# The FFN up projection of a hybrid diffusion trunk as a Strassen block product over pairs of token chunks

## The chip, the cores and the metric

One NeuronCore of one Trainium2 chip runs the kernel. The metric is the device time of one execution in microseconds, the median of three runs. Engines: PE multiplies matrices (PEld are its weight loads), DVE, ACT and POOL work elementwise on SBUF and PSUM, SP issues nearly all DMAs.

## The reference

One layer of a trunk with 128 context and 2048 latent tokens of width 1024, fp32. What matters here is the feed-forward block at its end, with FF = 2816:

```python
D_MODEL = 1024
D_FF = 2816
...
h = modulate(xs, g_norm2[l], sh2, sc2)
xs = xs + gt2[:, None, :] * conv_ffn(h, w_up[l], conv_w[l], conv_b[l], w_down[l])
...
#   x = x + gate2 * (SiLU(g) * val) @ w_down,  [g | val] = centred depthwise conv3(h @ w_up)
```

Context and latent tokens are separate sequences for the convolution. So `w_up` is 1024 x 5632: 22 blocks of 128 gate features and 22 of 128 value features, over 2176 tokens; the convolution takes each feature with its two neighbours in the token direction.

## The kernel before, in words

Every large product is made of three fp32r matmuls on hi/lo halves of the operands (`mm3`, L269 to L274): high by high, high by low, low by high. A half pair is made by an ACT copy to fp32r (the high half) and a DVE subtraction (the low half).

The kernel runs in stages: input projection with adaLN, state-space scan and attention, state-space output, merge, FFN up, FFN down. An instruction scheduler places each engine's instructions, from a program written stage by stage, so work of one stage may stand among another's.

The merge (`merge` L1010) goes over 17 tiles of 128 tokens. `turned` (L967) transposes the state-space half of a tile on PE (L972) and splits it (L974, L975); `merge_ssm` (L1045) multiplies by `wo` (24 matmuls of 512 columns, L273) and adds the result into x on DVE and POOL (L1053 to L1055); `h2_tile` (L1073) normalizes (`modulated_`, L246: L254 on DVE, transposes L259 on PE, modulation L265 on ACT) and `h2_split` (L1060) splits the tile into chunks H2 of 436 tokens plus a neighbour on each side: chunks 0 to 2 stay in SBUF, the tiles of chunks 3 and 4 go to DRAM (`hd`) and are split once the merge's memory is free. After ten tiles `merge` loads the first up weights.

`ffn_up` (L1089) takes 22 feature blocks fb times 5 chunks c. A pair of weight blocks [1024, 128], gate and value, is loaded and split once (`up_weights` L1080, L1085 on ACT, L1086 on DVE; 44 in all). One (fb, c) is two products of 24 matmuls over 438 columns (436 in the last chunk), 48 matmuls; 5280 in all. Each PSUM result becomes a convolution by three taps: ACT L1106, DVE L1108 and L1109; then tanh on ACT (L1112), two DVE products (L1113, L1114), and a DMA to `ffd` in DRAM. The first two feature blocks run over chunks 0 to 2 first, and stand partly in PE's gaps of the merge.

`ffn_down` (L1129) takes two halves of 11 feature blocks: 11 weight tiles (`down_weights`, L1125 and L1126), then per token tile a load from `ffd`, a split (L1139, L1140) and 66 matmuls of 512 columns in two or three banks, gated and added into x (L1152, L1153). `ffn_up` prepares the first `DW = 2` of its weights, and the gate rows of the down projection are made by PE transposes (`gate_rows`, L963).

```python
                    self.mm3(ps[:, :nn], lambda a, k: ws[fb][part][:, a, k, :],
                             lambda b, k: self.H2[c][:, b, k, :nn], 8)
```

## Time and profile before

| | |
|---|---|
| runs before | 2681.84, 2684.23, 2686.13 us; median 2684.23 |
| the profiled execution: span | 2684.1 us |
| PE busy, share of the span | 2531.3 us, 94% |
| PE weight loads | 2197.0 us, 82% |
| DVE | 1536.8 us, 57% |
| ACT | 1089.7 us, 41% |
| POOL | 727.8 us, 27% |

The profile shows one execution. An engine is busy while it executes an instruction; waiting, branching and issuing DMAs are not counted. The chain of waits goes back from the last instruction to whatever released each one. The clock granted to PE has two levels, 1.2 and 2.4 GHz; in the tables 1.00 is 2.4 GHz.

### The profile page before, as it was taken

The numbers are of one execution on the slowest core, as the hardware profiler recorded it, in microseconds if no ns is written. First come the engines' busy times: TensorE is split into PE (matmuls) and PEld (weight loads), VectorE is DVE, ScalarE is ACT, GpSimd is POOL, SyncE is SP. The second block draws the span as 40 slices with busy tenths as digits, with TensorE's granted clock in tenths as the row PEclk, the third lists the DMA queues.
The fourth block names the chain that finished last, engine by engine and source line by source line (L and its number), as shares of the span: only waits on it lengthen the run. The fifth ranks groups of instructions, "written<-read, shape, count | busy, mean of one in ns | idle before, by whom it ended". The sixth has DMA issues, their size and how long they took to land.

```text
span 2684.1 us, 34944 instructions
## 1 busy us (share of the span) xinstructions
PE 2531.3 (94%) x13046; PEld 2197.0 (82%) x13046; DVE 1536.8 (57%) x2576; ACT 1089.7 (41%) x2090; POOL 727.8 (27%) x1082
## 2 busy tenths in 40 slices
PE   6877997799999789999999999999999999999998
PEld 3756785688887567899999999999999988888887
DVE  6999767777776967654444444444444452224433
ACT  6544558777775666542222222222222230002111
POOL 1778105677776926500000000000000011111101
PEclk9988999899999899999999999999999999999999
DMA  8544745211112556641111111111111264344432
GB/s 247 166 144 159 231 133 188 93 66 66 66 62 80 123 181 223 215 154 55 40 55 40 40 55 40 55 40 40 55 39 48 61 202 132 107 131 139 124 115 74
DMA packets 245338, 287.20 MB, mean 107 GB/s; under 512 B 32058, under 2 KB 193202, under 8 KB 245042
## 3 DMA queue, kind: packets, MB, share of 16 engines
q1 hardware_dynamic: 240273, 276.07, 32.5%
q10 hardware_dynamic: 4896, 8.92, 1.0%
q8 instruction: 103, 1.69, 0.3%
q14 instruction: 66, 0.53, 0.1%
HBM read 183.08 MB, written 99.49 MB: 105 GB/s over the span
## 4 chain that ended last, share of the span: by engine, by line
PE 72%; DVE 6%; ACT 4%; issue 2%; DMA 1%; POOL 0%; SPq 0%; DVEq 0%; ACTq 0%; POOLq 0%
PE up L273 39%; PE dn L273 19%; PE pt L1003 3%; PE pm L273 2%; PE ps L851 2%; PE pt L879 2%; ACT HS L599 1%; PE po L883 1%; PE po L884 1%; DVE ha L682 1%; DVE pTl L890 1%; DVE sm L853 1%; DVE z L692 1%; ACT sm L840 0%; PE pst L596 0%
## 5 line engine op out<-in xcount | busy, mean ns | idle before, releaser
L273 PE MATMUL up<-H,upw 128*128 128x438 f32 (+1 forms) x5280 | 1058.9, 362 | 0.0
L273 PEld LDWEIGHTS up<-H,upw 128*128 128x128 f32 x5280 | 993.3, 188 | 61.0
L1108 DVE SCALAR_TENSOR_TENSOR cv<-up,vec,cv 128x436 f32<-128x436 f32 (+1 forms) x220 | 147.6, 671 | 455.9 <-ACT cv L1106 455.9
L1106 ACT ACTIVATE cv<-up,vec 128x436 f32<-128x436 f32 (+1 forms) x220 | 157.1, 714 | 575.1 <-PE up L273 575.1
L273 PE MATMUL dn<-dnw,aT 128*128 128x512 f32 (+1 forms) x1653 | 381.2, 386 | 0.0
L1153 POOL TENSOR_TENSOR xd<-xd,td 128x512 f32<-128x512 f32 x34 | 46.2, 1362 | 1225.5 <-DVE td L1152 1225.5
L273 PEld LDWEIGHTS dn<-dnw,aT 128*128 128x128 f32 x1653 | 307.7, 188 | 62.9
L1152 DVE TENSOR_TENSOR td<-dn,gate 128x512 f32<-128x512 f32 (+1 forms) x69 | 46.9, 683 | 288.4 <-PE dn L273 288.4
L187 DVE SCALAR_TENSOR_TENSOR wacc<-wa,scf,wacc 128x256 f32<-128x256 f32 x224 | 164.9, 777 | 10.1 <-ACT wacc L189 5.6
L1139 ACT ACTIVATE aT<-a 128x1408 fp32r<-128x1408 f32 x34 | 47.0, 1383 | 272.7 <-PE dn L273 261.2
L1109 DVE SCALAR_TENSOR_TENSOR cv<-up,vec,cv 128x436 f32<-128x436 f32 (+1 forms) x220 | 147.7, 671 | 7.5
L273 PE MATMUL dn<-upw,aT 128*128 128x512 f32 (+1 forms) x624 | 150.0, 385 | 0.0
L890 DVE TENSOR_TENSOR pTl<-pt,pTh 128x512 fp32r<-128x512 f32 x158 | 108.1, 684 | 51.7 <-ACT pTh L889 50.4
L273 PEld LDWEIGHTS dn<-upw,aT 128*128 128x128 f32 x624 | 115.6, 188 | 23.4
L853 DVE CUSTOM_DVE_ANT_0 sm<-ps,mask,nsink 128x640 f32<-128x640 f32 (+2 forms) x136 | 112.7, 830 | 29.7 <-PE ps L851 29.5
L840 ACT ACTIVATE sm<-sm,nm 128x640 f32<-128x640 f32 (+2 forms) x136 | 107.6, 791 | 27.4 <-DVE nm L853 27.2
L1112 ACT ACTIVATE th<-cv 128x436 f32<-128x436 f32 (+1 forms) x110 | 62.6, 569 | 135.1 <-DVE cv L1109 135.1
L1263 PE MATMUL aq<-win,hT 128*128 128x512 f32 x408 | 117.2, 423 | 0.0
L265 ACT ACTIVATE h<-tp,modc,G 128x128 f32<-128x128 f32 x272 | 100.1, 465 | 38.0 <-PE tp L259 33.5
L617 POOL TENSOR_TENSOR fm<-HS,A 128x544 f32<-128x544 f32 x64 | 91.8, 1435 | 86.5 <-ACT HS L599 70.7
L1263 PE MATMUL au<-win,hT 128*128 128x512 f32 x408 | 107.1, 405 | 7.1 <-DVE hT L1194 5.0
L879 PE MATMUL pt<-ident,sm 128*128 128x128 f32 x632 | 101.1, 279 | 12.4 <-ACT sm L840 7.6
(440 smaller groups left out, 3956.5 us busy)
## 6 DMA issues: line engine op xcount, KB each, us to landing
a<-ffd SPq DMA_DIRECT2D x34, 704.0 KB, 4.6
upraw<-in_w_up_dram SPq DMA_DIRECT2D x44, 512.0 KB, 3.8
ffd<-th SPq DMA_DIRECT2D x88, 218.0 KB, 1.9
xd<-x1d SPq DMA_DIRECT2D x34, 512.0 KB, 5.0
wa<-in_w_ada_dram SPq DMA_DIRECT2D x64, 256.0 KB, 3.1
dnraw<-in_w_down_dram SPq DMA_DIRECT2D x22, 512.0 KB, 5.2
qtd<-qT SPq DMA_DIRECT2D x17, 512.0 KB, 2.6
qT<-qtd SPq DMA_DIRECT2D x17, 512.0 KB, 3.9
```

The lines of the kernel that those rows point to most:

```text
L187: V.scalar_tensor_tensor(o, raw[:, k % RK], g, o, op0=OP.mult, op1=OP.add)
L265: S.activation(h[:, kk, :], pss[b][:, k, :], AF.Identity, scale=G[:, kk, st:st + 1], bias=self.modc[:, sh0 + kk, st:st + 1])
L273: self.T.matmul(ps, lhs(a, k), rhs(b, k), start=(first and k == 0 and n == 0), stop=(last and k == nk - 1 and n == 2))
L617: e.tensor_tensor(m, ev[:, :, ::-1] if n else ev, A[n], op=OP.mult)
L840: S.activation(out[hh][:, :W], out[hh][:, :W], AF.Exp, scale=-1.0, bias=nm[:, hh:hh + 1], accum_out=l[:, hh:hh + 1])
L853: V.tensor_tensor_reduce(t[:, :W], ps[:, c0:c0 + W], mask, -1.0, self.nsink[:, h:h + 1], op0=OP.add, op1=OP.min, accum_out=nm[:, hh:hh + 1])
L879: T.transpose(pt[:, hh], sm[hh][:, j * 128:(j + 1) * 128], self.ident)
L890: V.tensor_tensor(lo, pv, hi, op=OP.subtract)
L1106: S.activation(t[:, :n], ps[:, 1:1 + n], AF.Identity, scale=self.cw[1][:, j:j + 1], bias=self.cb[:, j:j + 1])
L1108: V.scalar_tensor_tensor(t[:, :n], ps[:, 0:n], self.cw[0][:, j:j + 1], t[:, :n], op0=OP.mult, op1=OP.add)
L1109: V.scalar_tensor_tensor(t[:, :n], ps[:, 2:2 + n], self.cw[2][:, j:j + 1], t[:, :n], op0=OP.mult, op1=OP.add)
L1263: T.matmul(t, hT[:, a, k, :], w[:, k, b, c0:c0 + t.shape[1]], start=(k + a + b == 0), stop=(k == 7 and a == 1))
```

## The change

The product [2176 tokens x 1024] by [1024 x 5632] becomes a block product. The operands of one unit are the four weight blocks a11, a12 (gate features, lower and upper half of the 1024 rows) and a21, a22 (value features), each 512 x 128, and the token blocks of two neighbouring chunks of 363 tokens (366 columns with their neighbours), each in two halves of the rows. Four block products would need 8 half products; the Strassen form (Winograd's, with 7) needs sums of the blocks of either side ahead, and sums of the products behind. Six chunks make three passes c of two chunks; 3 passes x 22 feature blocks are 66 units of 7 products of 12 matmuls over 366 columns, 5544 in all.

- `merge` (now L1017) no longer splits h; `h2_tile` (L1073) writes it to `hd` in DRAM, now [128, 8, 2184]. From tile 7 on it issues the token sums of pass 0 (`combos`), the operands of unit 0 and five of the seven token operands.
- `combos` (L1103): for each of four quarters, loads two chunks into a staging buffer, four POOL sums of 366 columns by L1114 to L1117, and a store to `td` in DRAM. Four steps a pass.
- `operand` (L1121): loads one of the seven token operands of a pass from `td` or `hd` by way of the same two staging buffers and splits it, in two instructions each of 2 x 366 columns on ACT (L1136) and DVE (L1137).
- `up_operands` (L1149): loads the two weight blocks of a feature block, four POOL sums S0 to S3 (L1155 to L1158) and seven splits of 512 elements: high halves on ACT (L1162), low halves (L1163) on DVE, one (`WP7`) on POOL. It does so in each unit.
- `ffn_up` (L1167): the products, copies of partial sums (`snap`, ACT), three DVE sums (L1237, L1246, L1258), the taps, and the gated product, whose last factor is a POOL product (L1199) as the value half of the convolution's vectors has been scaled by 0.5 in `vectors2`. PE's order in it is written by hand. At fb 18 and 21 of the first two passes the operands of the next pass are loaded.
- The down projection's pools open when those of the up projection are closed. Its weights are all loaded there, the gate rows come from DRAM (`gd`) by DMA, and the first token tile is loaded ahead of the weights.

The core of the diff:

```diff
+TOKENS = ((0, 0), (0, 2), (1, 1), (1, 0), (1, 2), (1, 3), (0, 3))
+WB7, WP7 = 9, (5,)
...
+        for o in (94, 138, 182, 226):
+            V.tensor_scalar(self.vec[:, o:o + 22], self.vec[:, o:o + 22], 0.5, None, op0=OP.mult)
...
+            if i == 7:
+                todo = self.combos(0)
+            if 7 <= i < 11:
+                next(todo)
+            if i == 8:
+                more = self.up_operands(0)
+            if 9 <= i < 16:
+                wts = next(more)
+            if 11 <= i < 16:
+                toks.append(self.operand(0, i - 11))
...
+    def combos(self, p):
+        G, Q = self.G, self.Q
+        for k in range(4):
+            t = self.stg.tile([128, 4, NR], F32, name="stg", bufs=2)
+            o = self.stg.tile([128, 4, NR], F32, name="stg", bufs=2)
+            for h in range(2):
+                c = NO * (2 * p + h)
+                Q.dma_start(t[:, h::2, :NI], self.hd.rearrange("q (b k) c -> q b k c", b=2)[:, :, k, c:c + NI])
+            tt = G.tensor_tensor
+            n = slice(0, NI)
+            tt(o[:, 0, n], t[:, 1, n], t[:, 0, n], op=OP.subtract)
+            tt(o[:, 1, n], t[:, 3, n], o[:, 0, n], op=OP.subtract)
+            tt(o[:, 2, n], t[:, 3, n], t[:, 1, n], op=OP.subtract)
+            tt(o[:, 3, n], t[:, 2, n], o[:, 1, n], op=OP.subtract)
+            Q.dma_start(self.td[p].rearrange("m q k c -> q m k c")[:, :, k], o[:, :, :NI])
+            yield
...
+    def operand(self, p, j):
+        n = 7 * p + j
+        pool, bufs = (self.tA, 5) if n % 9 < 5 else (self.tB, 4)
+        t = pool.tile([128, 2, 4, NR], F32R, name="T", bufs=bufs)
+        kind, m = TOKENS[j]
+        raw = self.stg.tile([128, 4, NR], F32, name="stg", bufs=2)
+        if kind:
+            self.Q.dma_start(raw[:, :, :NI], self.td[p, m])
+        else:
+            kh, h = divmod(m, 2)
+            c = NO * (2 * p + h)
+            self.Q.dma_start(raw[:, :, :NI], self.hd[:, 4 * kh:4 * kh + 4, c:c + NI])
+        for k in (0, 2):
+            src = raw[:, k:k + 2, :NI]
+            self.S.activation(t[:, 0, k:k + 2, :NI], src, AF.Copy)
+            self.V.tensor_tensor(t[:, 1, k:k + 2, :NI], src, t[:, 0, k:k + 2, :NI], op=OP.subtract)
+        return t
...
+    def up_operands(self, fb):
+        S, V, G, p = self.S, self.V, self.G, self.upw
+        g, v = self.up_raw(fb)
+        a11, a12, a21, a22 = g[:, 0:4], g[:, 4:8], v[:, 0:4], v[:, 4:8]
+        s = [p.tile([128, 4, 128], F32, name=f"S{n}", bufs=1) for n in range(4)]
+        G.tensor_tensor(s[0], a21, a22, op=OP.add)
+        G.tensor_tensor(s[1], s[0], a11, op=OP.subtract)
+        G.tensor_tensor(s[2], a11, a21, op=OP.subtract)
+        G.tensor_tensor(s[3], a12, s[1], op=OP.subtract)
+        out = []
+        for n, x in enumerate((a11, a12, s[1], s[0], s[2], a22, s[3])):
+            w = p.tile([128, 2, 4, 128], F32R, name="w", bufs=WB7)
+            S.activation(w[:, 0], x, AF.Copy)
+            (G if n in WP7 else V).tensor_tensor(w[:, 1], x, w[:, 0], op=OP.subtract)
+            out.append(w)
+            yield out
...
+    def ffn_up(self, first, p, pp):
+        Q, S, V, G = self.Q, self.S, self.V, self.G
+        units = [(c, fb) for c in range(3) for fb in range(22)]
+        o = slice(0, NO)
+        toks = {(0, j): t for j, t in enumerate(first[0])}
+        for j in range(5, 7):
+            toks[0, j] = self.operand(0, j)
+        wts = {0: first[1]}
+        for _ in first[2]:
+            pass
+        banks = {}
+        def product(u, j, bank, first=False):
+            w, t = wts[u][j], toks[units[u][0], j]
+            for k in range(4):
+                for n, (a, b) in enumerate(((0, 0), (0, 1), (1, 0))):
+                    self.T.matmul(bank[:, :NI], w[:, a, k], t[:, b, k, :NI], start=(first and k + n == 0),
+                                  stop=(k == 3 and n == 2), skip_group_check=True)
+        def taps(src, part, fb, name):
+            j = part * 22 + fb
+            t = p.tile([128, NO], F32, name=name, bufs=2)
+            S.activation(t, src[:, 1:1 + NO], AF.Identity, scale=self.cw[1][:, j:j + 1], bias=self.cb[:, j:j + 1])
+            V.scalar_tensor_tensor(t, src[:, 0:NO], self.cw[0][:, j:j + 1], t, op0=OP.mult, op1=OP.add)
+            V.scalar_tensor_tensor(t, src[:, 2:2 + NO], self.cw[2][:, j:j + 1], t, op0=OP.mult, op1=OP.add)
+            return t
+        def gated(g, v, c, fb):
+            th = p.tile([128, NO], F32, name="th", bufs=2)
+            S.activation(th, g, AF.Tanh, scale=0.5)
+            V.scalar_tensor_tensor(th, th, 1.0, g, op0=OP.add, op1=OP.mult)
+            G.tensor_tensor(th, th, v, op=OP.mult)
+            Q.dma_start(self.ffd[fb, :, NO * c:NO * c + NO], th)
+        def snap(x, name):
+            s = p.tile([128, NR], F32, name=name, bufs=2)
+            S.activation(s[:, :NI], x[:, :NI], AF.Copy)
+            return s
+        def begin(u):
+            x = pp.tile([128, 512], F32, name="X", bufs=3)
+            product(u, 0, x, True)
+            banks[u] = x, snap(x, "s1")
+        todo = []
+        begin(0)
+        for u, (c, fb) in enumerate(units):
+            x, s1 = banks.pop(u)
+            nxt = self.up_operands(units[u + 1][1]) if u + 1 < len(units) else iter(())
+            if fb in (4, 8, 12, 16) and c < 2:
+                if fb == 4:
+                    todo = self.combos(c + 1)
+                next(todo)
+            y = pp.tile([128, 512], F32, name="Y", bufs=2)
+            z = pp.tile([128, 512], F32, name="Z", bufs=3)
+            refill = fb == 21 and c < 2
+            def step(j):
+                for w in (next(nxt, None),):
+                    if w:
+                        wts[u + 1] = w
+                if refill and j is not None:
+                    toks[c + 1, j] = self.operand(c + 1, j)
+            if fb == 18 and c < 2:
+                for j in range(2):
+                    toks[c + 1, j] = self.operand(c + 1, j)
+            product(u, 1, y, True)
+            step(None)
+            V.tensor_tensor(y[:, :NI], y[:, :NI], s1[:, :NI], op=OP.add)
+            g1 = taps(y, 0, fb, "g1")
+            product(u, 2, x)
+            s2 = snap(x, "s2")
+            step(2)
+            product(u, 3, z, True)
+            step(3)
+            product(u, 4, x)
+            s3 = snap(x, "s3")
+            V.tensor_tensor(s3[:, :NI], z[:, :NI], s3[:, :NI], op=OP.add)
+            step(4)
+            v2 = taps(s3, 1, fb, "v2")
+            if u + 1 < len(units):
+                begin(u + 1)
+            step(None)
+            product(u, 5, x)
+            step(5)
+            v1 = taps(x, 1, fb, "v1")
+            gated(g1, v1, 2 * c, fb)
+            product(u, 6, z)
+            step(6)
+            V.tensor_tensor(z[:, :NI], z[:, :NI], s2[:, :NI], op=OP.add)
+            g2 = taps(z, 0, fb, "g2")
+            gated(g2, v2, 2 * c + 1, fb)
+            step(None)
+            wts.pop(u)
...
+        nxt = None if half else load(0)
+        w = [self.down_weights(half, k, rp, wp) for k in range(11)]
```

PE in the merge, around its last tiles. Before (`up` is the up projection, `pm` the merge's product, `tp` the transposes):

```order
L972 MATMUL tp<-ident,mo 128x128 x4
L273 MATMUL up_12860<-H_1_11262,upw 128x438
L273 MATMUL pm<-wo,oT 128x512 x2
L259 MATMUL tp<-ident,xn 128x128 x4
L273 MATMUL pm<-wo,oT 128x512 x2
L259 MATMUL tp<-ident,xn 128x128 x4
L273 MATMUL pm<-wo,oT 128x512 x20
```

Up matmuls stand among the merge's there. PE at the end of the merge after the change (`X` and `Y` are the PSUM banks of the first unit, `T` a token operand, `w` a weight operand):

```order
L280 MATMUL pm<-wo,oT 128x512 x4
L1097 MATMUL tp<-ident,xn 128x128 x4
L280 MATMUL pm<-wo,oT 128x512 x20
L1097 MATMUL tp<-ident,xn 128x128 x16
L1184 MATMUL X<-T,w 128x366 x12
L1184 MATMUL Y<-T,w 128x366 x12
```

No up matmul stands before the last transpose of the merge. DVE in the up stage, before (`cv0` and `cv1` are gate and value):

```order
L1108 SCALAR_TENSOR_TENSOR cv1_14636<-up1_14611,vec_153,cv1_14636 128x436
L1109 SCALAR_TENSOR_TENSOR cv1_14636<-up1_14611,vec_153,cv1_14636 128x436
L1114 SCALAR_TENSOR_TENSOR th_14640<-th_14640,cv1_14636 128x436
L1108 SCALAR_TENSOR_TENSOR cv0_14670<-up0_14645,vec_153,cv0_14670 128x433
L1109 SCALAR_TENSOR_TENSOR cv0_14670<-up0_14645,vec_153,cv0_14670 128x433
L1086 TENSOR_TENSOR upw_15035<-upraw_15033,upw_15035 128x1024
```

DVE in a unit after the change, from the low half of S0 (w3) on, up to that of a11 (w0) of the next feature block:

```order
L1163 TENSOR_TENSOR w_14958<-S0_14895,w_14958 128x512
L1191 SCALAR_TENSOR_TENSOR g1_14907<-Y_14877,vec_155,g1_14907 128x363
L1198 SCALAR_TENSOR_TENSOR th_14872<-th_14872,g2_14868 128x363
L1192 SCALAR_TENSOR_TENSOR g1_14907<-Y_14877,vec_155,g1_14907 128x363
L1163 TENSOR_TENSOR w_14980<-S2_14897,w_14980 128x512
L1198 SCALAR_TENSOR_TENSOR th_15002<-th_15002,g1_14907 128x363
L1246 TENSOR_TENSOR s3_14955<-Z_14878,s3_14955 128x366
L1163 TENSOR_TENSOR w_15019<-S3_14898,w_15019 128x512
L1191 SCALAR_TENSOR_TENSOR v2_14961<-s3_14955,vec_155,v2_14961 128x363
L1192 SCALAR_TENSOR_TENSOR v2_14961<-s3_14955,vec_155,v2_14961 128x363
L1163 TENSOR_TENSOR w_15058<-upraw_15046,w_15058 128x512
```

Six weight halves, three sums and the second tap of v2 from SBUF are new in a unit. POOL, before, goes from the merge's last sums straight to the down projection's:

```order
L1055 TENSOR_TENSOR mx__12555<-mx__12555,p1_12553 128x512 x2
L232 TENSOR_SCALAR ssq_12694<-ssq_12694 128x1
L234 TENSOR_TENSOR rstd_12697<-ssq_12694,mhalf_76 128x1
L1153 TENSOR_TENSOR xd_20010<-xd_20010,td_20012 128x512 x2
L1153 TENSOR_TENSOR xd_20092<-xd_20092,td_20094 128x512 x2
```

POOL after the change, in the same unit as DVE above:

```order
L1155 TENSOR_TENSOR S0_15050<-upraw_15048 128x512
L1199 TENSOR_TENSOR th_14872<-th_14872,v2_14806 128x363
L1156 TENSOR_TENSOR S1_15051<-S0_15050,upraw_15046 128x512
L1157 TENSOR_TENSOR S2_15052<-upraw_15046,upraw_15048 128x512
L1163 TENSOR_TENSOR w_14995<-upraw_14893,w_14995 128x512
L1158 TENSOR_TENSOR S3_15053<-upraw_15046,S1_15051 128x512
L1199 TENSOR_TENSOR th_15002<-th_15002,v1_14998 128x363
```

The sums for the unit after the next and the products of this unit alternate; each S buffer is single, so S0_15050 takes the memory of S0_14895, which DVE's first row above reads.

## Rows read from the trace of the kernel before

**Rows 1.** Busy time by stage; columns: window, length, engines (instructions), granted clock, DMA share, GB/s.

```profile
978.00:1171.00 193.00, 183.55 (x932) 154.84 (x930) 123.54 (x173) 109.71 (x255) 95.12 (x119) 0.99 0.62 209
1171.00:2168.00 997.00, 997.00 (x4994) 939.66 (x4993) 460.71 (x673) 256.35 (x363) 0.00 (x0) 1.00 0.17 53
2168.00:2684.00 516.00, 509.01 (x2277) 422.56 (x2275) 182.37 (x193) 89.94 (x123) 72.05 (x86) 1.00 0.40 126
978.00:1000.00 22.00, 18.75 (x86) 14.65 (x84) 8.30 (x14) 8.01 (x19) 10.35 (x18) 0.92 0.61 197
```

**Rows 2.** The chain of waits at its end; columns: start, us, engine, tile, line, instructions.

```profile
1169.14 1.75 PE dn L963 x16
1170.88 996.99 PE up L273 x4992
2167.87 509.15 PE dn L273 x2277
```

**Rows 3.** Groups of the up stage (1171 to 2168): busy us, mean ns | idle before.

```profile
L273 PEld LDWEIGHTS up<-H,upw 128*128 128x128 f32 x4990 | 939.3, 188 | 57.3
L1106 ACT ACTIVATE cv<-up,vec 128x436 f32<-128x436 f32 x164 | 117.1, 714 | 433.3 <-PE up L273 433.3
L1109 DVE SCALAR_TENSOR_TENSOR cv<-up,vec,cv 128x436 f32<-128x436 f32 x165 | 110.9, 672 | 5.7
L1114 DVE SCALAR_TENSOR_TENSOR th<-th,cv 128x436 f32<-128x436 f32 x83 | 50.9, 613 | 2.8
L1086 DVE TENSOR_TENSOR upw<-upraw,upw 128x1024 fp32r<-128x1024 f32 x40 | 48.8, 1220 | 23.5 <-ACT upw L1085 23.5
```

**Rows 4.** Timeline of PE at the end of the input projection; start, us, engine, line, operation.

```profile
408.58 1.78 PE L1263 MATMUL akv<-win,hT 128*128 128x256 f32 x13
410.20 0.28 PE L197 MATMUL rows<-whl,sel 128*16 128x256 f32 x1
```

**Rows 5.** Groups of the whole run, DVE and ACT in the down projection.

```profile
L1153 DVE TENSOR_TENSOR xd<-xd,td 128x512 f32<-128x512 f32 x33 | 22.8, 692 | 1.1
L1139 ACT ACTIVATE aT<-a 128x1408 fp32r<-128x1408 f32 x34 | 47.0, 1383 | 272.7 <-PE dn L273 261.2 <-issue 6.5 <-DMA a<-ffd 5.0
L1125 ACT ACTIVATE dnw<-dnraw 128x1024 fp32r<-128x1024 f32 x16 | 16.5, 1055 | 10.3 <-DMA dnraw<-in_w_down_dram 10.3
```

**Rows 6.** Timeline of the merge, DVE and POOL at three places.

```profile
1102.82 1.29 POOL L1055 TENSOR_TENSOR mx__12227<-mx__12227,p 128x512 f32<-128x512 f32 x1
1102.87 1.79 DVE L1054 TENSOR_TENSOR p<-p,gate 128x512 f32<-128x512 f32 x1
...
1133.48 0.75 DVE L254 TENSOR_SCALAR xn<-mx__12392,rstd 128x1024 f32<-128x1024 f32 x1
1133.64 1.74 POOL L1055 TENSOR_TENSOR mx__12474<-mx__12474,p 128x512 f32<-128x512 f32 x1 [0.41 <-DVE p L1054]
...
1015.21 0.74 DVE L1053 SCALAR_TENSOR_TENSOR upraw<-pm,rq,upraw 128x512 f32<-128x512 f32 x1
1015.87 0.68 DVE L975 TENSOR_TENSOR oT<-tp,oT 128x512 fp32r<-128x512 f32 x1
1015.96 1.28 POOL L1055 TENSOR_TENSOR mx__11471<-mx__11471,upraw 128x512 f32<-128x512 f32 x1
```

**Rows 7.** Up projection in the merge (columns PE, PEld, DVE, ACT), two transposes of the timeline.

```profile
1003.80:1133.00 129.20, 34.58 (x157) 29.14 (x157) 7.99 (x12) 4.26 (x6) 1.00 0.65 220
1133.00:1170.90 37.90, 27.31 (x132) 24.82 (x133) 6.71 (x10) 4.29 (x6) 1.00 0.49 179
...
1003.84 0.60 PE L972 MATMUL tp<-ident,mo 128*128 128x128 f32 x4
1133.02 0.60 PE L972 MATMUL tp<-ident,mo 128*128 128x128 f32 x4
```

**Rows 8.** The page's DMA issues: source, count, KB each, median us to landing.

```profile
dnraw<-in_w_down_dram SPq DMA_DIRECT2D x22, 512.0 KB, 5.2
upraw<-in_w_up_dram SPq DMA_DIRECT2D x44, 512.0 KB, 3.8
```

More of the change, by code (lines that the diff above doesn't have):

```diff
@@ L1023, in merge @@
                 self.h2_tile(i - 1, xs.pop(i - 1), p, pp)
-            if i == IU:
-                first = [self.up_weights(0, part, upw) for part in range(2)]
-            yield first
+            if i == 7:
[8 more added lines that the diff above has]
+                toks.append(self.operand(0, i - 11))
+        return toks, wts, more
     def merge_inputs(self, i, p, pp):
@@ L1418, in run @@
[L1418 to L1433 removed]
+            with fx, self.pool("tB") as self.tB, self.pool("upc") as p, self.pool("upps", space=PSUM) as pp:
+                with tc.manual_schedule(engines={ET.PE}):
+                    self.ffn_up(first, p, pp)
@@ L1436, in host_consts @@
+            for half in range(2):
+                self.ffn_down(half, gate, wp, rp, ap, tp, p, p2, dps)
 def host_consts():
```

179 lines of the change are left out of this document (71 added, 108 removed).

## The prediction

> **What bounds the kernel now.** I read first the table by stage [rows 1], then the chain of waits [rows 2], then the groups of the up stage [rows 3]. The table shows three stretches: the end of the merge (978 to 1171 us), the FFN up projection (1171 to 2168) and the down projection (2168 to 2684). In the middle one PE is busy for all of its 997.0 us, at a granted clock of 1.00, DVE for 461 and ACT for 256, and POOL does nothing. The chain agrees: its one step for the up projection is 996.99 us of PE for 4992 matmuls, with no wait in it, and a step of 509.15 us for the down projection follows at once. So a matmul of 437.6 columns on average costs 996.99 / 4992 = 199.7 ns, and what takes matmuls out of this stage comes back whole, until another engine becomes the limit.
>
> **PE's price.** The change has 5544 matmuls of 366 columns for 5280 of some 438. No row shows 366. Below stands the input projection: 13 matmuls of 256 columns in 410.20 - 408.58 = 1.62 us, 124.6 ns each [rows 4]; above, the 199.7 ns. On a line between them 366 columns cost 170.1 ns. That is 5544 x 0.1701 = 943 us of PE against 5280 x 0.1997 = 1054, so 111 us less. A unit (one feature block of one pass, 7 products of 12 matmuls) is 84 x 0.1701 = **14.29 us** of PE, 66 units in all.
>
> **DVE and POOL in a unit.** The weights were split once before; now they are summed and split again in each of the 66 units. DVE's durations lie on a line from 692 ns at 512 elements [rows 5] to 1220 at 1024 [rows 3]: 0.16 us + 1.035 ns an element. So a low half of 512 costs 0.69 us, an add of 366 0.54; a tap is 672 ns at 436 and so 0.60 at 363, a product with th 613 and so 0.54 [rows 3]. One unit has 6 low halves, 6 taps from PSUM, 3 adds from PSUM, 2 taps of a tile in SBUF (v2) and 2 th: 4.14 + 3.60 + 1.62 + 1.08 + 1.08 = **11.5 us** of DVE. POOL, idle before, has four weight sums and one low half of 512 at 1.29 us [rows 6] and two th products of 363 at 1.29 x 363 / 512 = 0.91: 8.3 us. ACT has 16 instructions (7 high halves, 3 copies of sums, 4 first taps, 2 tanh), none over the 0.71 of a tap at 436 [rows 3], so at most 11.4. Each alone fits under PE's 14.29.
>
> They do not run alone. In rows 6 POOL's add runs from 1102.82 to 1104.11, and DVE's product of two SBUF tiles, issued at 1102.87, ends at 1104.66: 0.55 after POOL, as if it had run only then. The other way round DVE is done at 1134.23 and POOL's add ends at 1135.38, 1.15 later. A DVE row that takes one input from PSUM (L975) takes 0.68 us with POOL running beside it, and follows its neighbour with an overlap of 0.08. The Trainium skill, page "SBUF — State Buffer", section "Who interferes with whom", has a rule that speaks against this change: the port pair that DVE and GpSimd share is an exclusive lock held for a whole instruction, and a DVE instruction with two SBUF inputs contends with a GpSimd one that reads SBUF. The trace agrees with it [rows 6]; without it, DVE's 11.5 us would lie beside POOL's 8.3, PE would set the pace, and the time would be A's below.
>
> Ten of a unit's DVE instructions read SBUF alone (6 low halves, 2 th, 2 taps of v2), and all seven of POOL. As the change orders them, POOL's S0 waits for the buffer that DVE's low half of the old S0 (w3) frees, and from there the two alternate: S0 1.29, th 0.40, POOL's th 0.77, w4 0.55, S1 1.15, th 0.40, S2 1.15, w6 0.55, w5 on POOL 1.15, v2 tap 0.40, S3 1.15, v2 tap 0.40, w0 0.61 = 9.97 us. (0.55 and 1.15 are those of rows 6, taken to 363 or 366 columns by 1.035 ns an element on DVE and 1.29 / 512 us on POOL, w0 being 0.69 less the overlap of 0.08.) Three PSUM rows of DVE lie under POOL's. The other nine, v1's two taps, w1, the add into z, w2, g2's two taps, the add into y and w3, are 5.55 us, less nine overlaps of 0.08: 4.83, and I give 0.4 more to where they meet a POOL th or wait for ACT. The ring is **15.2 us**, 0.9 over PE. Its bounds: 14.29, when the collisions find gaps, and 16.2, when no neighbours overlap (0.7) and POOL's start adds 0.3. I take 15.2, since the order has each of POOL's sums wait for buffers that DVE frees: 66 x 15.2 = 1003 us against the 997 of before, **+6**.
>
> **Merge.** Up matmuls that filled the merge are gone: 157 between 1003.8 and 1133.0 and 132 after [rows 7], 31.4 and 26.4 us at 199.7 ns. Thirteen tiles lie between the two transposes of rows 7, 129.2 us; without the 31.4 a tile is 7.5 us. If PE's up work was the whole delay, and the 1.75 us of transposes for the down gate [rows 2], now a DMA, goes too, the merge ends at 1170.9 - 31.4 - 26.4 - 1.75 = 1111.3; if another engine set the pace, it still ends near 1171. New in it are 16 POOL sums of 366 for pass 0 (0.92 each, 14.7 us), first weights and five operands; two of DVE's H splits go. I add POOL's sums to the floor, 1126, as POOL has 95 us in that stretch beside DVE's 124 [rows 1]: **-45** (from -60 to 0). Two operands need the pool that opens after the merge, whose DMA, ACT and DVE nothing covers: +8; the last unit prepares no successor: -5. Together **+3**.
>
> **Pass changes.** Twice, seven operands are loaded and split anew, 14 low halves of 732 on DVE, 0.16 + 0.757 - 0.08 = 0.84 each, on the engine that is the ring's: 2 x 14 x 0.84 = **+24** (to 40, if the loads also wait). The sums for passes 1 and 2, 32 on POOL at 0.77 behind a DVE row, cost 25 us if all fall into the alternating part and 0 if into the nine rows' 5.2 us: **+12**.
>
> **Start of the down projection.** Before, two down weights and all operands were there and PE ran through [rows 2]. Now the last unit's tail (add 0.54, ACT 0.65, taps 1.2, th 0.5), the load and split of the first 128 tokens (ACT 1.38, DVE as much) and one weight (1.06) [rows 5] lie open: some 7 us. After such a pause PE may be granted 1.2 instead of 2.4 GHz for a while: in the 22 us that open the merge's stretch, where PE starts with gaps, the mean granted clock is 0.92 [rows 1], which is 2 us more: **+9** (4 to 25). Later weights come within 2 us each, below PE's 4 banks x 3 matmuls of 509.15 / 2277 = 0.224 us a k [rows 2], so the rest stays at 516 us. The vectors' four tiny scalings and the gate's DMA cost nothing: SP's queue is at a share of 0.17 in the up stage, and PE covers the gate's loads.
>
> **Sum:** -45 + 6 + 3 + 24 + 12 + 9 = +9, on a span of 2684.1 us, which is 0.1 below the median of 2684.2: **2693 us**. With each term at its bounds this case holds 2660 to 2730.
>
> **Rivals.**
> A, faster: the ports collide less than the order makes it seem, and PE sets the pace at 14.29 us. For it: DVE's 11.5 us and seven chance collisions (10 SBUF rows of 0.58 in 14.3 us catch each with 0.4, 0.6 us each) make 13.4, below PE. Against it: S0 and S1 wait for buffers, so collisions aren't chance. Then 66 x 14.29 is 54 us less than 997, the combos are hidden and the rest stays: -45 - 54 + 3 + 24 + 0 + 9 = -63, **2621 us**.
> B, slower: the pass change is bound by its loads. All operands and combos go through two staging buffers; seven operands are 7 x 750 KB, and a load of 512 KB takes 3.8 or 5.2 us to land [rows 8], so up to 7.6 for 750 KB. If they follow each other with the splits behind them, a change costs 7 x 7.6 = 53 us and a little less under cover, 42 instead of 12: +30 each, **2753 us**. It decides once a buffer's load and split exceed what PE has left of the unit, 14.29 us for five. For it: both buffers are taken by the combos of the same pass. Against: two operands come three units earlier, and DMA's share is 0.17.
> C, the change doesn't do what it says: matmuls don't get cheaper with their columns, since each weight load takes 188 ns [rows 3]. Then a unit is 84 x 0.188 = 15.8 us, +39 over 15.2: **2732 us**. Against: the 124.6 ns of rows 4, with weight loads alike.
>
> **Chances.** The forecast 0.54, A 0.27, B 0.14, C 0.05. A's own range is 2600 to 2645, B's 2735 to 2790. To leave out 2 in 10, the range takes most of A and B: 2615 to 2760. A measurement of this kernel can tell 0.2% from no change, 2679 to 2690: of the forecast's own 2660 to 2730, a fifth lies there and a fifth below. So faster is 0.27 + 0.11 = 0.38, same 0.11, slower 0.54 - 0.22 + 0.14 + 0.05 = 0.51.
>
> **What would show it.** Right: in the up stage PE busy below 0.96, units 15.2 us apart, the chain passing between DVE and POOL at L1155 to L1163, DVE's SBUF rows longer by half beside POOL, the two pass changes as gaps of PE of 10 to 20 us, merge's end at 1126. A: PE busy throughout, one chain step on L1184. B: gaps of 40 us at the changes, released by DMA. C: 188 ns a matmul with PE full. I'm wrong in the sum if the merge doesn't shorten, or if ACT or DVE in a unit are longer than rows of before give them.

## The result, and the profile after

The changed kernel takes 2798.36 us (median of 4 runs, 2797.43 to 2802.10) against 2683.19 (2681.84 to 2686.13) for the kernel before: **4.3% slower**, ratio 1.0426, 95% interval 1.0411 to 1.0440. The forecast was 2693, its range 2615 to 2760: the direction was right, the size wrong. The profiled execution has a span of 2796.8 us, 112.7 more than before. A run below that has no interval was executed once.

The table by stage answers to [rows 1]; its four stretches are the end of the merge, the up projection to the end of its last product, the pause of PE before the down projection, and the down projection.

```profile
core 0: us, PE busy (x) PEld busy (x) DVE busy (x) ACT busy (x) POOL busy (x), PEclk, DMA share, GB/s
978.00:1189.70 211.70, 146.37 (x616) 111.75 (x617) 99.32 (x121) 100.34 (x242) 115.45 (x144) 0.85 0.84 247
1189.70:2248.60 1058.90, 956.08 (x5544) 934.13 (x5544) 1036.41 (x1274) 565.60 (x1077) 675.03 (x483) 0.99 0.36 110
2248.60:2265.20 16.60, 0.03 (x1) 0.00 (x0) 4.86 (x6) 4.90 (x6) 1.90 (x2) 0.64 1.03 331
2265.20:2796.80 531.60, 524.35 (x2277) 426.01 (x2277) 182.75 (x193) 90.50 (x123) 72.11 (x86) 0.99 0.39 126
```

| stage | before | after | difference | forecast for it |
|---|---|---|---|---|
| up projection starts at | 1170.9 | 1189.7 | +18.8 | -45, and +8 for two operands |
| up projection | 997.0 | 1058.9 | +61.9 | +6 - 5 + 24 + 12 |
| pause before the down projection | 0 | 16.6 | +16.6 | +9 |
| down projection to the end | 516.2 | 531.6 | +15.4 | 0 |

The four differences add up to 112.7. The first one missed by 56 us, more than half of the whole miss of 104; the up projection missed by 25, the pause by 8 and the down projection by 15.

**The up projection.** DVE is now busy for 1036 of 1059 us, PE for 956. The chain of waits of one unit, which [rows 2] showed as one step of PE, is DVE's, with steps put down to nothing:

```profile
1816.97 1.09 DVE w L1163
1818.07 0.45 DVE th L1198
1818.52 1.03 issue
1819.54 0.53 DVE s L1246
1820.07 1.25 DVE w L1163
1821.32 1.56 DVE v L1191
...
1822.97 1.38 issue
1824.35 0.68 DVE w L1163
...
1832.56 1.10 DVE w L1163
```

The same row, w4 (the low half of S2), comes again after 1832.56 - 1816.97 = **15.59 us**; the ring was forecast at 15.2, with 16.2 as its upper bound. The timeline of POOL and DVE in another unit shows how the two alternate:

```profile
1705.74 1.29 POOL L1155 TENSOR_TENSOR S<-upraw 128x512 f32<-128x512 f32 x1 [2.68 <-DVE w L1163]
1706.10 1.34 DVE L1198 SCALAR_TENSOR_TENSOR th<-th,g 128x363 f32<-128x363 f32 x1
...
1708.44 1.75 POOL L1156 TENSOR_TENSOR S<-S,upraw 128x512 f32<-128x512 f32 x1
...
1708.95 1.63 DVE L1198 SCALAR_TENSOR_TENSOR th<-th,g 128x363 f32<-128x363 f32 x1
...
1710.14 1.59 POOL L1157 TENSOR_TENSOR S<-upraw 128x512 f32<-128x512 f32 x1
1710.50 0.53 DVE L1246 TENSOR_TENSOR s<-Z,s 128x366 f32<-128x366 f32 x1
1710.95 1.33 DVE L1163 TENSOR_TENSOR w<-S,w 128x512 fp32r<-128x512 f32 x1
...
1713.87 1.51 DVE L1192 SCALAR_TENSOR_TENSOR v<-s,vec,v 128x363 f32<-128x363 f32 x1
```

POOL's sum takes 1.29 us where DVE is out of its way and 1.59 to 1.75 after a DVE row; th takes 1.34 and 1.63 where the stand-alone price was 0.54. A DVE row with an operand in PSUM (L1246) still takes its 0.53 between them, beside POOL's sum. This is the lock that the Trainium skill, page "SBUF — State Buffer", section "Who interferes with whom", describes; the trace agrees. From S0 at 1705.74 to the end of v2's last tap at 1715.38 the two need 9.6 us, where the forecast had 9.4 (9.97 less w0). DVE's busy time counts this waiting (the same th row is 0.52 us long in the run without the sums, below), so its 1036 us are no measure of its own work.

**Merge and pause.** Two rows of the merge's waits (us in all, times, longest): ACT waits for the store of h, DVE for POOL's norm.

```profile
ACT h L1100 <- DMA hd<-h: 53.7, 14, 5.5
DVE xn L1093 <- POOL rstd L241: 46.9, 14, 9.5
```

The timeline of DVE (start, us, ...) has the first and the last tile normalised:

```profile
1006.60 0.75 DVE L1093 TENSOR_SCALAR xn<-mx__11290,rstd 128x1024 f32<-128x1024 f32 x1 [0.46 <-POOL rstd L241]
...
1183.65 0.75 DVE L1093 TENSOR_SCALAR xn<-mx__12616,rstd 128x1024 f32<-128x1024 f32 x1 [9.54 <-POOL rstd L241]
```

The timeline of ACT at the start of the down projection shows that it splits the second token tile ahead of the first weight, and waits 7 us for it:

```profile
2254.45 1.38 ACT L1281 ACTIVATE aT<-a 128x1408 fp32r<-128x1408 f32 x1 [2.64 <-DMA a<-ffd]
2262.84 1.38 ACT L1281 ACTIVATE aT<-a 128x1408 fp32r<-128x1408 f32 x1 [7.01 <-DMA a<-ffd]
2264.12 3.88 ACT L1269 ACTIVATE dnw<-dnraw 128x1024 fp32r<-128x1024 f32 x4
```

From the start of the down projection the chain of waits is one step of PE to the last product:

```profile
2265.22 524.36 PE dn L280 x2277
```

### The profile page after: what moved, and what is told of

Its sections match the earlier page's. It is cut to its first block, busy times and chain, and to the rows that moved or that the text cites. A ratio compares the mean times of both kernels' runs of the same rounds, so it can differ in the third digit from the quotient of the medians.

```text
span 2796.8 us, 38074 instructions
## 1 busy us (share of the span) xinstructions
PE 2459.6 (88%) x13294; PEld 2146.5 (77%) x13294; DVE 2090.3 (75%) x3138; ACT 1394.2 (50%) x2802; POOL 1422.9 (51%) x1592
## 5 line engine op out<-in xcount | busy, mean ns | idle before, releaser
L1184 PE MATMUL X<-T,w 128*128 128x366 f32 x3168 | 568.3, 335 | 101.4 <-ACT s L1204 98.1
L1184 PEld LDWEIGHTS X<-T,w 128*128 128x128 f32 x3168 | 537.9, 192 | 122.1 <-ACT s L1204 118.3
L280 PE MATMUL dn<-dnw,aT 128*128 128x512 f32 (+1 forms) x2277 | 524.3, 393 | 16.6 <-ACT dnw L1269 16.6
L1184 PE MATMUL Z<-T,w 128*128 128x366 f32 x1584 | 286.8, 330 | 4.7 <-DVE s L1246 4.7
L1163 DVE TENSOR_TENSOR w<-S,w 128x512 fp32r<-128x512 f32 x264 | 287.7, 1093 | 2.0 <-ACT w L1162 1.9
L1184 PEld LDWEIGHTS Z<-T,w 128*128 128x128 f32 x1584 | 267.9, 189 | 6.0 <-DVE s L1246 5.9
L1199 POOL TENSOR_TENSOR th<-th,v 128x363 f32<-128x363 f32 x132 | 136.3, 1033 | 215.5 <-DVE v L1192 159.0
L1162 ACT ACTIVATE w<-S 128x512 fp32r<-128x512 f32 x264 | 164.1, 625 | 56.4 <-PE Z L1184 36.1
L1198 DVE SCALAR_TENSOR_TENSOR th<-th,g 128x363 f32<-128x363 f32 x132 | 178.8, 1355 | 5.8 <-ACT th L1197 5.8
L1155 POOL TENSOR_TENSOR S<-upraw 128x512 f32<-128x512 f32 x66 | 91.9, 1393 | 151.9 <-DVE w L1163 122.3
L1184 PE MATMUL Y<-T,w 128*128 128x366 f32 x792 | 144.0, 331 | 0.0
L860 DVE CUSTOM_DVE_ANT_0 sm<-ps,mask,nsink 128x640 f32<-128x640 f32 (+2 forms) x136 | 112.7, 830 | 28.9 <-PE ps L858 28.7
```

What stands on the lines that cost most here:

```text
L280: self.T.matmul(ps, lhs(a, k), rhs(b, k), start=(first and k == 0 and n == 0), stop=(last and k == nk - 1 and n == 2))
L860: V.tensor_tensor_reduce(t[:, :W], ps[:, c0:c0 + W], mask, -1.0, self.nsink[:, h:h + 1], op0=OP.add, op1=OP.min, accum_out=nm[:, hh:hh + 1])
L1155: G.tensor_tensor(s[0], a21, a22, op=OP.add)
L1162: S.activation(w[:, 0], x, AF.Copy)
L1163: (G if n in WP7 else V).tensor_tensor(w[:, 1], x, w[:, 0], op=OP.subtract)
L1184: self.T.matmul(bank[:, :NI], w[:, a, k], t[:, b, k, :NI], start=(first and k + n == 0), stop=(k == 3 and n == 2), skip_group_check=True)
```

## Experiments: the up projection

**The sums on DVE.** The busiest engine gets four instructions more in each unit.

```diff
-        G.tensor_tensor(s[0], a21, a22, op=OP.add)
+        V.tensor_tensor(s[0], a21, a22, op=OP.add)
...
```

(and so for S1 to S3)

> The four weight sums S0 to S3 of a unit run on DVE instead of POOL; nothing else changes. Theory (DVE and POOL take turns at SBUF, so each POOL sum of 512 costs the ring its whole length): four POOL rows of 1.6 us leave the ring and four DVE rows of 0.6 enter it; a unit falls from 15.57 us to PE's 14.0 to 14.4, the up stage from 1051 to 950 to 975 us, the whole to about 2710. Rival (DVE's own work sets the pace, since DVE is busy 1033 of the stage's 1051 us): DVE gets 4 x 0.6 us more in each unit, 18 us a unit, and the whole comes to about 2950.

2723.88 us, ratio 1.0152 (1.0133 to 1.0170). The table for its up projection:

```profile
1190.40:2175.40 985.00, 951.79 (x5544) 931.30 (x5544) 969.61 (x1530) 574.61 (x1081) 308.00 (x227) 0.99 0.39 118
```

985 us instead of 1058.9, though DVE now has 1530 instructions for 1274; its busy time falls to 970 us. The rival is out by 200 us. A unit takes 14.39 us in the steady state, inside what the theory gave; the stage is 10 us above it and the whole 14, as the units around the token sums and pass changes take up to 19 us. POOL keeps w5 and two th products, which DVE still meets; PE alone needs 14.05, as the next run shows.

**The sums left out.**

```diff
-        G.tensor_tensor(s[0], a21, a22, op=OP.add)
...
-        for n, x in enumerate((a11, a12, s[1], s[0], s[2], a22, s[3])):
+        for n, x in enumerate((a11, a12, a21, a22, a11, a22, a12)):
```

> The four weight sums are left out altogether: the products that used sums use single blocks of the weights (the up projection's values are then other ones). Theory of the turns: POOL keeps one low half and two products a unit, and a unit falls to PE's 14.0 us, the up stage to about 950, the whole to about 2695. Rival (the hand-overs between PE and ACT set the 15.57 us, as PE's idle time before its products is put down to ACT's copies): a unit stays at 15.3 us or more.

```profile
1194.20:2144.00 949.80, 935.42 (x5541) 931.87 (x5542) 791.60 (x1273) 592.12 (x1077) 263.76 (x227) 0.99 0.41 122
```

949.8 us for the stage, 2694.05 for the whole: PE sets the pace with 14.05 us a unit, and DVE's 1273 instructions take 792 us where 1274 of the same kinds took 1036. The 245 us between are waiting behind POOL. With it the hand-overs to ACT are out as a cause.

## Experiments: the merge

**No up matmuls in it.** The kernel before, with

```diff
+            ups = st.enter_context(self.pool("upps", bufs=2, space=PSUM))
```

moved from ahead of the merge to behind it.

> The kernel before, with the PSUM banks of the up projection opened only after the merge, so that PE has no up matmuls to fill the merge with. It measures what the merge takes without them. My prediction's step: the merge ends 58 us earlier, near 1113 us, and the whole stays at 2684 to 2690. Rival (the merge is bound by its chain of ACT, DVE and loads, and the up matmuls lay in gaps): it ends at 1150 or later, and the whole is 35 to 60 us longer.

2711.94 us. Its chain's end:

```profile
1135.88 1057.83 PE up L273 x5280
2193.72 509.13 PE dn L273 x2277
```

Between the two expectations: the fill's 57.8 us had cost the merge 35.0 (1170.9 - 1135.9) and lain in gaps for 23. So the changed kernel had 35 us to win there, not 59.6, and its start at 1189.7 has **53.8 us** of new delay in it.

**Halves of h.** Three half buffers instead of one whole.

```diff
-        h = p.tile([128, 8, 136], F32, name="h", bufs=1)
+        hs = [p.tile([128, 4, 136], F32, name="h", bufs=3) for _ in range(2)]
```

> In the merge the buffer h is cut into halves of four row blocks with a store of its own for each, and three such halves rotate instead of one whole buffer; same work. Theory (the single h buffer is held until its store has landed, 53.7 us of ACT's waiting): this waiting falls below 15 us and the up projection starts some 40 us earlier, near 1150 instead of 1189.7. Rival (the DMA engines are full, share 0.92 from 1084 to 1189 us): the start moves by less than 10 us, and the waiting turns up at other loads.

2806.18 us, the up projection starts at 1194.1. ACT's wait for the store is gone, and others stand in its place. The first row is the changed kernel's wait for the transposes, the others are this run's:

```profile
ACT h L1100 <- PE tp L1097: 25.0, 4, 9.9
...
ACT h L1102 <- PE tp L1099: 54.0, 8, 10.8
...
ACT T L1139 <- DMA stg<-hd: 16.1, 1, 16.1
POOL stg L1117 <- DMA stg<-hd: 14.2, 4, 5.3
```

My theory of the single buffer fell: the wait with the largest sum was not what set the end. The rival's signs came instead: the start moved by 4 us only, and waits for loads turned up. ACT's row that waits 16.1 us for a load stands in its order in front of rows that the tiles need; that this sets the end is not shown.

**Preparation written behind the merge**, with one h or with halves.

```diff
-            if i == 7:
-                todo = self.combos(0)
...
+        for _ in self.combos(0):
+            pass
+        more = self.up_operands(0)
...
```

> The changed kernel, with the token sums of pass 0, the first weights and the first five operands written behind the merge instead of among its tiles; the merge still stores h to DRAM through one buffer. Theory A (what the merge lost is this preparation, whose loads hold up the in-order queues of POOL and ACT that the tiles need): the last transposes of the merge come at 1136 to 1146 us instead of 1185, near those of the kernel before without up matmuls. Theory B (the store of h out of one buffer is the loss): they stay at 1165 or later. Either way the preparation then lies open, some 40 us, before the first product.

> As the run with the preparation behind the merge, and h in three rotating halves. Theory A: little more than without the halves, the last transposes at 1130 to 1142 us. Theory B: they come 20 us or more earlier than with the single buffer.

2803.87 and 2802.21 us, up projection at 1196.1 and 1191.5. Neither tests the theories: the scheduler set the rows among the tiles again, since nothing kept them from it.

**Preparation kept out by memory.** The staging buffers in memory that the merge frees.

```diff
-            self.stg = fx.enter_context(self.pool("stg", side="right"))
...
+            self.stg = fx.enter_context(self.pool("stg"))
+            for _ in self.combos(0):
+                pass
+            for j in range(5):
+                first[0].append(self.operand(0, j))
```

> The changed kernel, with the staging buffers in memory that the merge frees, so that the token sums and operands of pass 0 cannot start before the merge's last products; the run with the preparation merely written behind the merge did not test this, since the scheduler put it among the tiles again. The weights of unit 0 stay in the merge. If the preparation (its loads, or the waits for them in the queues of POOL and ACT) is what the merge lost, its last transposes come at 1136 to 1146 us instead of 1185; if the store of h is, at 1165 or later. The preparation then lies open before the first product, 40 to 60 us by its 12 MB and 0.3 MB a us of DMA and the work behind them.

2826.29 us.

```profile
1170.13 1.97 PE L1091 MATMUL tp<-ident,xn 128*128 128x128 f32 x8 [7.48 <-DVE xn L1087]
1206.87 0.67 PE L1178 MATMUL X<-T,w 128*128 128x366 f32 x1 [34.77 <-ACT T L1130]
```

The last transposes come 14 us earlier, at 1170, far from 1136 to 1146; sums and operands among the tiles are not the bulk. Laid open, they cost 35 us of idle PE.

**Transfers without the work.** For pass 0 no sums and splits, the loads straight into the operands.

```diff
+            if p == 0:
+                Q.dma_start(self.td[p].rearrange("m q k c -> q m k c")[:, :, k], t[:, :, :NI])
+                yield
+                continue
```

> The changed kernel with the transfers of the preparation of pass 0 (chunks to the staging buffer, to td, and into the operands) but without its sums on POOL and its splits on ACT and DVE: the operands of pass 0 hold high halves alone, unsummed, and the sums for the later passes are left out too, so the up projection's values are other ones. If the DMA engines are the limit in the merge (share 0.92), the last transposes stay at 1175 us or later; if the waits of POOL's and ACT's queues for those transfers are, they come at 1150 or earlier.

2788.95 us, the last transposes at 1191 us. The rows for 1084 to 1150, first the changed kernel's, then this run's (the last two columns are the DMA share and GB/s):

```profile
1084.00:1150.00 66.00, 45.09 (x185) 34.12 (x186) 26.58 (x35) 30.79 (x77) 42.81 (x55) 0.85 1.02 304
...
1084.00:1150.00 66.00, 43.88 (x167) 33.62 (x165) 20.59 (x29) 25.14 (x64) 22.21 (x35) 0.77 1.06 310
```

The DMA engines are full in both, the store of h lands in 9.0 us instead of 6.8, and without the work the merge is as late: by the expectation, the transfers alone hold it there. Against that stands the run with the preparation kept out by memory, whose share is 0.81 in these 66 us and whose merge is only 14 us earlier. Which of the two, transfers or waits, binds in the changed kernel is not shown.

**Larger pieces.** h in DRAM with a token's four row blocks side by side.

```diff
-            self.hd = dp.tile([128, 8, 2184], F32, name="hd")
+            self.hd = dp.tile([128, 2, 4 * 2184], F32, name="hd")
...
-            src = raw[:, k:k + 2, :NI]
+            src = raw.rearrange("q (c k) -> q k c", k=4)[:, k:k + 2]
```

> The changed kernel with the layout of h in DRAM turned so that a token's four row blocks lie together: the store of a tile is 2 pieces of 2 KB on each partition instead of 8 of 512 bytes, an operand's load 1 piece of 5.9 KB instead of 4 of 1.5 KB, and the token sums go by quarters of the columns instead of by row block. Bytes, sums and splits are the same; ACT writes h and reads the staging buffer with a step of 16 bytes. If the DMA engines' work on small pieces is what stretches the merge (the late-preparation run put its last transposes at 1170 us with the store alone, 1130 without either), the last transposes come at 1165 us or earlier instead of 1184.5, and the store lands in 5 us or less instead of 6.8. If it is the bytes, or the wait of the tile behind its store, less than 8 us change.

2818.39 us. The store lands in 3.4 us, as expected, but the last transposes come at 1187.8; by its own expectation, not the cause alone. The step of 16 bytes has a price of its own in the splits (732 elements), in the groups by line for 1190 to 2250 us (busy us, mean ns | idle):

```profile
L1139 DVE TENSOR_TENSOR T<-stg,T 128x732 fp32r<-128x732 f32 x32 | 56.5, 1800 | 6.5 <-ACT T L1138 6.3
L1138 ACT ACTIVATE T<-stg 128x732 fp32r<-128x732 f32 x32 | 47.3, 1537 | 2.2 <-DMA stg<-hd 2.2
```

against 1188 and 812 ns in the changed kernel in the same stretch. The same together with the sums on DVE and the single token buffer (below):

> The turned layout, the weight sums on DVE and the single buffer of the down projection's tokens together. If the three add up: 2717 us of the run with the latter two, less what the layout gives in the merge (20 us or more if small pieces are the cause, under 8 if not), so 2697 or below against 2710 or above. The time of the kernel before, 2684, is reached only if the layout also shortens the changes between passes.

2725.55 us (ratio 1.0160, 1.0136 to 1.0183), no faster than without the layout.

**Weights held back, and everything late.** Every run of the changed kernel so far has its first tile normalised at 1001 to 1013 us, against 989 in the kernel before without the fill. No token sum stands there yet (the first starts at 1074); what does is the weights of units 0 and 1, on POOL and on DVE. POOL's first sum of either, in the changed kernel:

```profile
986.76 1.27 POOL L1155 TENSOR_TENSOR S<-upraw 128x512 f32<-128x512 f32 x1 [1.40 <-DMA upraw<-in_w_up_dram]
...
998.36 1.27 POOL L1155 TENSOR_TENSOR S<-upraw 128x512 f32<-128x512 f32 x1 [0.64 <-DVE w L1163]
```

A column copied into the weight buffer from a later tile holds them back.

```diff
+            if src is not None:
+                self.V.tensor_copy(r[:, 0, 0:1], src[:, 0:1])
```

"Everything late" is this and the edit that keeps sums and operands out by memory, together.

> The kernel with the sums on DVE and the single token buffer, in which the weight buffers of units 0 and 1 first take one column of a late merge tile, so that these weights cannot be prepared at the head of the merge: unit 0 after the ninth tile, unit 1 after the last. If the weights at the head delay the whole merge, the first tile is normalised at 989 to 993 us instead of 1006, the merge ends some 15 us earlier, and the whole is about 2700. If the merge catches up anyway, its end moves by less than 5 us. Second, read in the down projection alone: a pad of 128 bytes brings its weights to the address offset that they had before (224 instead of 96 above a multiple of 256); a bank of 33 matmuls takes 7.48 us if that offset makes the difference, 7.67 to 7.70 if not.

> The changed kernel with all preparation behind the merge: token sums and operands as in the late-preparation run, and the weights of units 0 and 1 gated by the last tile. The merge then does its own work and the store of h. If the head of the merge and the preparation among its tiles are the loss, the first tile comes at 989 to 993 us and the last at 1130 to 1138; if the store of h stretches the tiles too, the last comes at 1145 to 1155 (9.9 us a tile for 8.75). The preparation lies open behind it, 50 us or more.

> The same with the turned layout, whose store goes in pieces of 2 KB and lands in 3.4 us instead of 6.8. If the small pieces of the store are what stretches the tiles, 8.75 us a tile and the last at 1130 to 1138; if the store does so by its bytes or its place in SP's queue, no earlier than without the turned layout.

Held back alone, with the sums on DVE and the single token buffer: 2713.70 us (ratio 1.0109, 1.0093 to 1.0126). The first tile comes at 998.6 us and the last at 1183.4, against 1001.5 and 1175.9 in the same kernel without the gating (the run with four banks set aside, below): the head gains 3 us and the end loses 8. With everything late, 2818.05 and, in large pieces, 2826.97 us; their last tiles come later than the 1155 and the 1138 that were expected at the latest. The starts of the normalisation of a tile, from the timeline:

| run | tile 1 | tile 14 | us a tile | tile 17 |
|---|---|---|---|---|
| before, no fill | 989.2 | 1105.2 | 8.9 | 1129.4 |
| everything late, large pieces | 997.2 | 1110.5 | 8.7 | 1150 |
| everything late | 992.4 | 1120.3 | 9.8 | 1164 |
| late sums and operands | 1010 | 1140 | 10.0 | 1169 |
| changed kernel | 1006.6 | 1140 | 10.3 | 1183.7 |

(In the two with everything late the weights come among the last three tiles, as the held column had landed by then; they are read up to tile 14.) So of the 54 us, by the differences between these runs, 14 stand at the head (1006.6 less 992.4: the weights), some 0.9 us a tile, 15 in all, come from the store in pieces of 512 bytes, and the other 25 from the rest of the preparation, above all among the last three tiles, which take 43.6 us in the changed kernel and 24.1 in the kernel before without the fill. With all of it late and the pieces large, a tile takes 8.7 us up to tile 14, as without the fill. The single shares are argued, not shown: removed one by one, the parts moved the last transposes by anything from 14 us earlier to 8 later.

## Experiments: the down projection

**ACT's order, and PSUM banks.** With the sums on DVE, a single buffer for the token tiles, and four banks set aside.

```diff
-            a = ap.tile([128, 11, 128], F32, name="a", bufs=2)
+            a = ap.tile([128, 11, 128], F32, name="a", bufs=1)
...
+            pad = st.enter_context(self.pool("pad", space=PSUM))
```

> The kernel with the sums on DVE, with two edits in the down projection, each read at its own place. First, the buffer of the token tiles from DRAM is single, so that ACT splits the first weights before the second token tile: if the start waits for ACT's order, the pause of PE shrinks from 16 to about 8 us; if for the DMA engines, it stays. Second, its PSUM tiles lie in banks 4 to 7, as before, instead of 0 to 3: a bank of 33 matmuls takes 7.48 us as in the kernel before if the banks make the difference, 7.67 if not.

2717.21 us.

```profile
2178.83 1.22 PE L280 MATMUL dn<-dnw,aT 128*128 128x512 f32 x2 [7.29 <-ACT dnw L1269]
2180.68 6.74 PE L280 MATMUL dn<-dnw,aT 128*128 128x512 f32 x18 [0.63 <-DVE dnw L1270]
```

PE's idle time falls from 16.1 us, in the run with the sums on DVE alone, to 7.3: ACT's order was 9 us of the pause. Little of it reaches the end: from the last up product on, this run takes 543.9 us against 547.2, since PE's first 20 matmuls run with gaps, at a granted clock of 0.66 over 10 us, and then wait 1.4 us for the next token tile. The pace is 7.70 us a bank of 33 matmuls: not the banks.

**A pad of 128 bytes.** What moved in memory between the kernels are the down weights, the moving operand of these matmuls: they began 224 bytes above a multiple of 256, and now 96. The gated run had, besides,

```diff
+            ap.tile([128, 32], F32, name="pad", bufs=1)
```

Rows of the first half of the down projection (two banks a tile), in the kernel before, in the changed kernel and in the gated run:

```profile
2384.97 0.69 DVE L1152 TENSOR_TENSOR td<-dn,gate 128x512 f32<-128x512 f32 x1 [4.00 <-PE dn L273]
2392.38 0.69 DVE L1152 TENSOR_TENSOR td<-dn,gate 128x512 f32<-128x512 f32 x1 [6.72 <-PE dn L273]
2399.93 0.69 DVE L1152 TENSOR_TENSOR td<-dn,gate 128x512 f32<-128x512 f32 x1 [4.00 <-PE dn L273]
...
2390.67 0.69 DVE L1304 TENSOR_TENSOR td<-dn,gate 128x512 f32<-128x512 f32 x1 [6.90 <-PE dn L280]
2398.41 0.69 DVE L1304 TENSOR_TENSOR td<-dn,gate 128x512 f32<-128x512 f32 x1 [4.20 <-PE dn L280]
2406.01 0.69 DVE L1304 TENSOR_TENSOR td<-dn,gate 128x512 f32<-128x512 f32 x1 [6.91 <-PE dn L280]
...
2388.44 0.69 DVE L1309 TENSOR_TENSOR td<-dn,gate 128x512 f32<-128x512 f32 x1 [6.72 <-PE dn L280]
2395.99 0.69 DVE L1309 TENSOR_TENSOR td<-dn,gate 128x512 f32<-128x512 f32 x1 [4.01 <-PE dn L280]
2403.40 0.69 DVE L1309 TENSOR_TENSOR td<-dn,gate 128x512 f32<-128x512 f32 x1 [6.72 <-PE dn L280]
```

7.74 and 7.60 us in the changed kernel against 7.55 and 7.41 in the gated run, the kernel before's own figures: 0.19 us a bank, over 68 banks (17 tiles, two halves, two banks) **12.9 us**. To see whether it was the gating, the same version without it (sums on DVE, a single buffer for the token tiles, the pad), and to see whether other operands behave so, the kernel before with other rows for its moving operand:

> The changed kernel with the weight sums on DVE, the single token buffer and the pad of 128 bytes, without the gating of the weights. If the three add up as the stages say: 2717 us of the run with the first two less 12.6, so 2704; the merge, the changes between passes and DVE's pace in a unit stay as they are. Rival: the pace of the down projection was the gating's doing, and the whole stays at 2716.

> The kernel before, with the rows of its H chunks 0, 1 and 3 at a step of 448 elements (1792 bytes, 7 x 256) instead of 438 (1752), so that all their moving operands begin 224 bytes above a multiple of 256, as the down projection's do; chunks 2 and 4 keep theirs (a scratch tile of the merge is halved to make room). If the offset sets PE's pace, a product of 24 matmuls over 438 columns on chunks 0, 1 and 3 takes some 4.70 us (24 x (182.5 + 13.4) ns, the down projection's overhead) instead of 4.79, chunks 2 and 4 stay, and the whole is 10 to 14 us faster than the kernel before. If it does so for the down projection alone, nothing moves.

The first, without the gating, has the same pace, 7.55 and 7.41, and takes 2707.63 us (ratio 1.0085, 1.0068 to 1.0103): the best version of the change that I found, and still slower than the kernel before. Its up projection is 984.2 us, 13 less than before; it starts 22 us later, and what follows it is 13 us longer. The second, whose edit is `[128, 2, 8, {2: 438, 4: 436}.get(c, 448)]` for the shape of H2 and a scratch tile of half its size, takes 2683.73 us, ratio 1.0002 (0.9991 to 1.0012), and its products come every 4.74 and 4.86 us as before. So the place of the moving operand tells in the down projection (the pad moved nothing else that its matmuls read or write) and not in the up projection; why is open.

## Why the prediction was wrong

- **PE's price** was right: 12 matmuls of 366 columns take 2.01 us, 167 ns each, against 170; 84 of them are 14.05 us a unit against 14.29.
- **DVE and POOL in a unit**: the mechanism was right and is shown by two runs; the size was not. The ring is 15.57 us in the steady state for 15.2, so the term +6 measures +30.6 (66 x 15.57 = 1027.6 less 997.0), within its bounds, and the difference is the up projection's whole miss. The 1.15 us of a POOL sum behind a DVE row was read from a DVE row that has only one SBUF tile (L254); rows with two bear it out (S2 at 1710.14 ends 1.15 after th).
- **Pass changes, combos and the last unit**: +36 and -5 forecast, 1058.9 - 1027.6 = +31.3 measured. The parts differ: the units around the two changes are 17 and 7 us over their 15.57, those at the start of the first pass 5, and the last unit gives nothing back. Rival B, 40 us at each change, did not happen.
- **Merge**, the step that failed. "If PE's up work was the whole delay" took 59.6 us off and then put POOL's 14.7 on. The run without the fill shows 35.0 off. And the new work cost 53.8, not 14.7 + 8: the forecast priced its sums on POOL at their own duration, as if nothing queued behind them, gave the weights and five of the operands nothing, and gave the store of h, 17 tiles in pieces of 512 bytes for 7 in pieces of 4 KB, nothing either. It says nothing of the head of the merge, where the weights' rows stand ahead of the first tile's norm. How the 53.8 divide among these stays open.
- **Start of the down projection**: +9 forecast, 16.6 measured, within its bounds. The tail and the first load were in it; that ACT's next row is the second token tile, which waits for its DMA in a pause with 331 GB/s of transfers, was not, and PE's idle time fell by 9 us when that order changed. The gate rows, put at nothing since PE would cover their loads, are loaded in this pause, 2 x 512 KB issued at 2248.66 (the 0.17 that the forecast gave to SP's queue is the DMA engines' share); what they cost was not tested.
- **The rest of the down projection** was put at nothing; 12.9 of its 15.4 us are PE's pace and went with the pad, the others lie at the start, where PE's granted clock is 0.74 over the first 10 us:

```profile
2265.20:2275.20 10.00, 9.98 (x32) 7.72 (x33) 7.03 (x7) 5.29 (x6) 0.00 (x0) 0.74 0.83 284
```

- **The range** was not the sum of its terms' bounds. Taken from the terms, the forecast's own case runs from -83 to +165 us, 2601 to 2849, not from 2660 to 2730; 2798 lies inside that. Even so the merge is outside its bounds: with the two operands it was given -52 to +8 and came to +18.8. (Rival A's 13.4 us are 13.2 by its own figures, which changes nothing.)
- That the direction came out right was luck for the most part: slower had a chance of 0.51, and the largest term, -45, had the wrong sign.
- Of the rivals, A (2621) is what the run without sums shows of the stage, and was wrong for this order; C was wrong. The forecast had no case in which the merge grows.

## What to carry to other kernels

When work is moved to an idle engine, ask which port it shares with the busy one: here moving four sums a unit from POOL to the engine that was "98% busy" saved 74 us, as part of that busy time was waiting. Work that a change frees from a stage is worth only what that stage waited for it (35 of 58 us), and preparation that is put into a stage can cost more than its own duration (here 54 us for work priced at 23). A range is to be added up from the bounds of its terms. A wait with a large sum is not the bound until its removal has been timed.

## What was not expected of the hardware

- 33 matmuls of 512 fp32r columns take 7.48 us (226.7 ns each) with the down weights 224 bytes above a multiple of 256, and 7.67 (232.4 ns) at 96, in PSUM banks 0 to 3 (7.70 in banks 4 to 7); in the up projection, rows at one offset or at many made no difference.
- A split of 732 elements read with a step of 16 bytes takes 1537 ns on ACT against 812, and 1800 on DVE against 1188 (waiting for POOL may be in both of DVE's).
- In the merge the store of 512 KB lands in 6.8 us in pieces of 512 bytes and in 3.4 in pieces of 2 KB, where the loads of the preparation had larger pieces too. With everything late it is 6.5 and 4.8.
